# Neighbourhood attention: the last row group's bias tables from the host, the middle row groups head by head, scaling taken off GpSimd, and operand splits kept out of the steps that add tables

## The chip, the core and the metric

The kernel runs on one core of one Trainium2 chip. The metric is the device time of one execution in microseconds (us); lower is better. Engines are named as the profile names them: PE is TensorE (PEld its weight loads), DVE is VectorE, ACT is ScalarE, POOL is GpSimd, SP is SyncE, which here issues nearly all DMAs.

## What is computed

One layer of a bidirectional encoder: RMSNorm, one input projection to q, k, v and a gate, 2-D neighbourhood attention with a learned position bias, the SiLU gate, one output projection, the residual, and a final RMSNorm. Cut to what matters:

```python
S, D, H, hd, GRID_W = 2048, 1024, 16, 64, 64       # 32 rows of 64 tokens
h = rmsnorm(x, norm_0)
q, k, v, gate = split(h @ w_in_0, 4)                # 1024 -> 4096
for r in range(32):                                 # each grid row; keys of 8 rows, 16 columns
    s = einsum(q[r], k[rows(r)]) / sqrt(hd)
    s = where(col_valid, s + bias(rpb_0, r), -1e30)
    o[r] = einsum(softmax(s), v[rows(r)])
x = x + (o * silu(gate)) @ w_out_0                  # 1024 -> 1024
out = rmsnorm(x, norm_f)
```

All arrays are float32.

## The kernel before

**Products.** Matrix operands are split into a high and a low part in the fp32r type: ACT writes the high part (a copy), DVE writes the low part (the difference of the source and the high part, two inputs in SBUF). Each product is then three matmuls. In `use_item` the splits of projection weights are tiles `w` (L178, L179) and those of `w_out` are `woh`, `wol` (L183, L184). `split_og` splits the gated attention output, tile `ograw`, into `gh`, `gl` (L1107, L1108).

**Stages.** Two stages of seven-product projections come first (L419, L540); the change leaves them alone. From then on attention and the rest run together, in the loop `for i in range(N + 2)` at the end of `build`, of 66 steps. Queries are cut into four row groups T = 0 to 3 of 8 grid rows, heads into eight pairs p, so there are 32 (p, T), in the order of the list `order`; each takes two steps, a step being two of the four column blocks C. Row groups 1 and 2 have the same bias and mask; 0 and 3 have their own. So there are three row types, in `ROW_TYPE`.

A step i issues to PE, in this order:
- *fill*: matmuls of the last projections (L363 to L367), and after those, of the output projection (L1242 to L1246). `amount[i]` says how many matmuls, about 15 in the first 48 steps and 20 after.
- the transposes of pair i-2 (L1015), into PSUM banks `ph`. DVE and ACT copy them out as `pta` (L1019, L1018).
- the scores of pair i (L978), 12 matmuls into four banks `s`. Of the eight banks some were `ph` or output banks just before, so the second half of the scores starts only once the copies above, or the evictions `y` (L1140), have emptied them.
- the products with v of pair i-2 (L1033).

DVE adds the table `em` to the scores and takes the maximum (L985, with the L985 read of the accumulator); ACT takes the exponential (L988); DVE the reciprocal of the sum (L994); POOL multiplies by it (L996, `normalise`); the transposes of the next step wait for that.

**Tables.** `bias(p, ty, cty)` makes the six tables `em` of a head pair and a row type: POOL adds the laid-out bias `e` (one DMA of 240 KB per head, `load_e`) and the mask `mk` (L960). `begin(i)` calls it in the even steps in which the pair's tables aren't there. In `order` the first five pairs have T = 1 and 2 next to each other, the other three have all T = 1 before all T = 2, and so add their tables twice.

**The rest of the work.** `consume` splits weights some way ahead, twice in each group of 24 fill matmuls. `outputs` loads `ograw`, splits it ahead (`ahead`, with the distance `near`), and after 24 matmuls `add_rows` adds the residual (L1140) and squares on ACT (L1143). `finish` then takes the root of the row's mean square on DVE, eight small instructions L1156 to L1163, scales the left half on DVE (L1170) and the right half by ACT and POOL (L1171, L1172), and stores. `run_roots` issues those when `quiet` is set, that is, in odd steps.

Everything is issued in an order that the program writes out: `clock` counts fill matmuls, `store(key, lag, f)` puts f off by so many of them, `due` runs what has come due. DMAs of SP go in order.

Of the kernel before, what the change touches and what calls it, by code (L numbers as in the profile page):

```python
# [10 lines left out]
F32 = mybir.dt.float32  # L11
# [27 lines left out]
MASK_N = [[(u1 - u0) * (v1 - v0) for v0, v1 in TYPE_COLS] for u0, u1 in TYPE_ROWS]  # L39
MASK_ALL = sum(sum(n) for n in MASK_N)  # L40
KINDS = {"q": 0, "k": 4, "v": 8, "g": 12}
# [26 lines left out]
@with_exitstack  # L68
def build(ctx, tc, x, xr, xt, wg, rpb, w_out, n0, nf, masks, out):
    nc = tc.nc  # L70
# [199 lines left out]
    def load_ahead():  # L270
        while state["loaded"] < min(len(items), state["used"] + AHEAD):
            load_item(items[state["loaded"]])
            state["loaded"] += 1

    def consume(n, asked=False):
        for _ in range(n):
            load_ahead()
            if state["used"] == len(items) or not may_use(items[state["used"]]):
                return
            if items[state["used"]][0] == "o" and clock[0] - asked_at[items[state["used"]]] < 32 and not asked:  # L280
                return
            it = items[state["used"]]
            state["used"] += 1
            use_item(it)
# [69 lines left out]
    def group(w, a, c, n):  # L354
        p = bank(512, "pp")
        for k in range(NK):
            if k in (3, 6):
                consume(1)
# [533 lines left out]
    LAST, stored_at = {}, {}  # L892
    order = [(p, 0) for p in range(NP)] + [(p, T) for p in range(5) for T in (1, 2)]
    order += [(p, T) for T in (1, 2) for p in range(5, NP)] + [(p, 3) for p in range(NP)]
    pairs = [(p, T, (h, h + 1)) for p, T in order for h in (0, 2)]
# [56 lines left out]
    def bias(p, ty, cty):  # L952
# [4 lines left out]
        for s in range(2):  # L957
            t = mp([128, 512], F32, "em")[:, :n]
            EM[p, ty, cty, s] = t
            (nc.gpsimd if attending[0] or not s else nc.vector).tensor_tensor(  # L960
                sh(t), E[p, s][:, u0 + 4:u1 + 4, v0 + 8:v1 + 8].rearrange("p u (s v) -> p s u v", v=8), sh(MK[0][:, m0:m0 + n]), OP.add)

    X, PT, O, ST = {}, {}, {}, {}
# [150 lines left out]
    squared = [0]  # L1114
    quiet = [False]

# [31 lines left out]
    def finish(n):  # L1148
# [16 lines left out]
        def scale():  # L1165
# [3 lines left out]
            else:  # L1169
                nc.vector.scalar_tensor_tensor(y[0], y[0], r, late["nf"][0], op0=OP.mult, op1=OP.mult)  # L1170
                nc.scalar.activation(y[1], y[1], AF.Copy, scale=r)  # L1171
                nc.gpsimd.tensor_tensor(y[1], y[1], late["nf"][1], OP.mult)  # L1172

# [28 lines left out]
    def outputs():  # L1202
# [6 lines left out]
        def ahead(k, i=0):  # L1209
# [7 lines left out]
            n = ready["split"]  # L1217
            near = 2 if quiet[0] else 1 if i >= 4 else 0
            if n < ready["loaded"] and place[n] <= k + near and clock[0] - loaded_at[n] >= 28 and whole(n):
# [44 lines left out]
    first = 8  # L1264
    amount = [(early - 3 * first) / 48] * 48 + [(384 - 30) / 18] * 18
    calm_debt = amount[0] / 2
# [32 lines left out]
    def begin(i):  # L1299
        all_loads()  # L1300
        m = i // 2
        if i % 2 == 0 and i < N:
            load_v(*order[m])
        if i % 2 == 0 and i < N:
            p, T = order[m]
            ty = ROW_TYPE[T]
            for key in [key for key in EM if key[:2] != (p, ty)]:
                del EM[key]
            for cty in range(3):
                if (p, ty, cty, 0) not in EM:  # L1310
                    bias(p, ty, cty)
            if m + 1 < len(order):
                nx = order[m + 1]
                kh, kl = load_k(*nx)
                if nx[0] != p:
                    later_loads(load_e(nx[0]), 5, 3)
# [15 lines left out]
    for i in range(N + 2):  # L1332
        a = amount[i]
        begin(i)
        feed(a * 0.25)
        quiet[0] = i % 2 == 1 or i >= N
        if quiet[0]:
# [3 lines left out]
        feed(a * 0.55, 8)  # L1341
        quiet[0] = i >= N
        if 0 < i <= N:
# [53 lines left out]
```

## Time and profile before

| what | before |
|---|---|
| median of 3 runs (lowest to highest) | 1088.14 us (1086.99 to 1088.67) |
| the profiled execution | 1090.37 us |
| its span, first to last instruction | 1088.6 us |
| PE busy in the span | 1071.1 us (98%) |
| DVE, ACT, POOL busy | 724.2, 531.8, 355.7 us |
| attention loop, from its first fill matmul to the last instruction | 528 us to 1088.6 us |
| DMA | 205.39 MB, 189 GB/s over the span |

The profile's lines read: source line, engine, operation, written tile, arrow, read tiles, size, count; then busy time, mean of one in ns, and after the bar the idle time just before them with what ended most of it. In the list of waits a line reads "engine and line that waited, the one waited for: us in total, times, longest". In the timeline it is start, duration, engine, instruction, count, and in brackets the idle time of that engine just before. The windows give each engine's busy time in a stretch, with the count of instructions started there, then PE's granted clock, the DMA share and GB/s.

A matmul of 512 columns is shown with 389 ns, but the next one starts about 227 ns after it: the shown ends overlap. So a pause of PE shows in the starts, not in the busy share.

### The profile page before, as it was taken

Reading aid. Unit: us, or ns where it says so; the run is one execution under the profiler, and the core shown is the slowest. Engines: PE = TensorE matmul, PEld = TensorE weight load, DVE = VectorE, ACT = ScalarE, POOL = GpSimd, SP = SyncE. Lnnn points to the kernel's source line nnn. Section 1 sums busy time; section 2 is a strip of 40 time slices with the busy share of each in tenths; the row PEclk is TensorE's granted clock in tenths of the full one; section 3 lists DMA queues with packets and bytes.
Section 4 is the critical chain, followed back from the end, with each engine's and each line's share of the span. In section 5 each row is a group of like instructions: output and inputs, shape, how many; then the busy total and the mean of one; then the engine's idle time right before and its main releaser. Section 6 shows DMA issues by size and latency. Waiting matters only on the chain. (4 is left out here: it accounts for less than half of the span.)

```text
span 1088.6 us, 21531 instructions
## 1 busy us (share of the span) xinstructions
PE 1071.1 (98%) x7621; PEld 875.0 (80%) x7621; DVE 724.2 (67%) x1680; ACT 531.8 (49%) x1260; POOL 355.7 (33%) x474
## 2 busy tenths in 40 slices
PE   9999999999999999999999999999999999999997
PEld 6888888887888888888878888888878787888885
DVE  5376888769897536565675566657786757766553
ACT  7545344333343334332465565657666555655431
POOL 0000322212220000000175665544477656557210
PEclk9999999999999999999999999999999999999999
DMA  8633565444555234445997778858986777776352
GB/s 307 216 97 106 195 202 182 125 136 148 146 167 148 83 87 135 116 131 170 283 278 209 241 222 241 276 169 246 287 264 208 236 254 206 251 224 221 103 153 77
DMA packets 125299, 205.39 MB, mean 189 GB/s; under 512 B 11336, under 2 KB 51528, under 8 KB 125192
## 3 DMA queue, kind: packets, MB, share of 16 engines
q1 hardware_dynamic: 125048, 203.76, 60.7%
q8 instruction: 60, 0.98, 0.4%
q14 instruction: 47, 0.39, 0.1%
q10 hardware_dynamic: 144, 0.26, 0.1%
HBM read 145.26 MB, written 58.72 MB: 187 GB/s over the span
## 5 line engine op out<-in xcount | busy, mean ns | idle before, releaser
L960 POOL TENSOR_TENSOR em<-e,mk 128x480 f32<-128x480 f32 (+5 forms) x160 | 134.4, 878 | 192.6 <-DVE u L432 189.8
L996 POOL TENSOR_SCALAR x<-x,st 128x360 f32<-128x360 f32 (+5 forms) x256 | 142.5, 577 | 163.3 <-DVE st L994 110.4
L419 PE MATMUL pp<-h,f 128*128 128x512 f32 x576 | 186.5, 389 | 0.0
L988 ACT ACTIVATE x<-x,st 128x360 f32<-128x360 f32 (+5 forms) x256 | 151.7, 594 | 54.7 <-DVE st L985 54.7
L419 PE MATMUL pp<-t,f 128*128 128x512 f32 x648 | 156.0, 390 | 0.3 <-DVE u L432 0.2
L439 POOL TENSOR_TENSOR tmp<-tmp,rb 128x512 f32<-128x512 f32 x36 | 58.5, 1625 | 271.1 <-DVE tmp L437 220.3
L419 PEld LDWEIGHTS pp<-t,f 128*128 128x128 f32 x648 | 121.5, 188 | 26.4 <-DVE u L432 1.2
L419 PEld LDWEIGHTS pp<-h,f 128*128 128x128 f32 x576 | 108.1, 188 | 22.5
L985 DVE CUSTOM_DVE_ANT_0 x<-s,em 128x360 f32<-128x360 f32 (+5 forms) x256 | 123.7, 539 | 3.5 <-PE s L978 1.8
L419 PE MATMUL pp<-l,f 128*128 128x512 f32 x288 | 112.0, 389 | 0.0
L1019 DVE COPY pta<-ph 120x384 f32<-120x384 f32 (+5 forms) x128 | 62.9, 516 | 63.2 <-PE ph L1015 62.6
L1246 PE MATMUL po<-wol,gh 128*128 128x512 f32 x252 | 100.7, 399 | 0.0
L1033 PEld LDWEIGHTS o<-pta,vt 120*64 120x64 f32 (+2 forms) x1792 | 84.6, 138 | 19.8 <-issue 15.6
L1242 PE MATMUL po<-woh,gh 128*128 128x512 f32 x252 | 99.7, 396 | 0.0
L1244 PE MATMUL po<-woh,gl 128*128 128x512 f32 x252 | 99.5, 395 | 0.0
L1018 ACT ACTIVATE pta<-ph 120x384 f32<-120x384 f32 (+5 forms) x128 | 52.3, 459 | 88.5 <-PE ph L1015 88.4
L1033 PE MATMUL o<-pta,vt 120*64 120x128 f32 (+5 forms) x1792 | 93.5, 256 | 1.5 <-DVE pta L1019 1.2
L978 PE MATMUL s<-kt,qh 64*128 64x480 f32 (+5 forms) x512 | 86.8, 379 | 6.0 <-DVE pta L1019 2.3
L540 PE MATMUL pv<-wh,h 128*128 128x512 f32 x256 | 88.1, 390 | 0.0
L540 PE MATMUL pv<-wl,h 128*128 128x512 f32 x256 | 87.9, 389 | 0.0
L540 PE MATMUL pv<-wh,l 128*128 128x512 f32 x256 | 87.9, 389 | 0.0
L402 DVE TENSOR_TENSOR f<-raw,f 128x512 fp32r<-128x512 f32 x90 | 69.9, 776 | 22.4 <-ACT f L401 22.4
(149 smaller groups left out, 1910.3 us busy)
## 6 DMA issues: line engine op xcount, KB each, us to landing
raw<-in_wg_dram SPq DMA_DIRECT2D x126, 256.0 KB, 4.6
e<-in_rpb_dram SPq DMA_DIRECT2D x54, 240.0 KB, 4.2
row<-in_xr_dram SPq DMA_DIRECT2D x32, 256.0 KB, 4.2
vd<-v SPq DMA_DIRECT2D x32, 256.0 KB, 2.7
k_hi<-hi SPq DMA_DIRECT2D x32, 256.0 KB, 3.2
k_lo<-lo SPq DMA_DIRECT2D x32, 256.0 KB, 2.9
sgd<-sg SPq DMA_DIRECT2D x32, 256.0 KB, 3.2
qr<-qd SPq DMA_DIRECT2D x32, 256.0 KB, 3.6
```

The costliest lines, as they stand in the source:

```text
L402: nc.vector.tensor_tensor(t[:, 1], src, t[:, 0].bitcast(F32), OP.subtract)
L419: nc.tensor.matmul(B[n, P], t[:, int(m == 2), c], x[k][int(m == 1)], start=P in (1, 6, 5) and k == 0 and m == 0, stop=k == 3 and m == 2, s ...
L540: nc.tensor.matmul(ps[t], a[:, o], b, start=k == 0 and m == 0, stop=k == NK - 1 and m == 2)
L960: (nc.gpsimd if attending[0] or not s else nc.vector).tensor_tensor(sh(t), E[p, s][:, u0 + 4:u1 + 4, v0 + 8:v1 + 8].rearrange("p u (s v) - ...
L978: nc.tensor.matmul(pst[s], qq[a, qs], kk[a, :r1 - r0, c0:c1].rearrange("p r (s c) -> p s r c", c=8), start=(m == 0), stop=(m == 2))
L985: nc.vector.tensor_tensor_reduce(X[i, C][s], pst[s], EM[p, ROW_TYPE[T], COL_TYPE[C], s], -1.0, 1e38, OP.add, OP.min, st[:, s:s + 1])
L988: nc.scalar.activation(X[i, C][s], X[i, C][s], AF.Exp, bias=st[:, s:s + 1], scale=-1.0, accum_out=st[:, 2 + s:3 + s])
L996: nc.gpsimd.tensor_scalar(X[i, C][s], X[i, C][s], st[:, 4 + s:5 + s], 0.5, op0=OP.mult, op1=OP.mult)
L1033: nc.tensor.matmul(o[s * 64:s * 64 + 64, C * 128 + q0:C * 128 + q0 + nq], vt[:k, strip, s * 64:s * 64 + 64], t[:k, at:at + nq], start=firs ...
L1242: nc.tensor.matmul(p, gh, woh[q, j], start=(i == 0), stop=False)
L1244: nc.tensor.matmul(p, gl, woh[q, j], start=False, stop=False)
L1246: nc.tensor.matmul(p, gh, wol[q, j], start=False, stop=(i == NK - 1))
```

## The change

The host now adds bias and mask for row type 2 and passes them as `last`, 960 columns for each head; `load_last` reads the six tables of a head pair straight into the tiles `em`, 960 KB in six DMAs where `load_e` read 480 KB in two, and POOL adds nothing for T = 3. The order has T = 1 and T = 2 next to each other for all eight pairs. `finish` scales both halves on DVE, with neither ACT nor POOL. `quiet` is set in every step in which `begin` added no tables, not in odd steps, and `consume` and `ahead` split only then (unless the operand is needed at once); a group has three calls of `consume` instead of two. The first 48 steps have 60 fill matmuls less, the last 18 have 60 more.

```diff
-order = [(p, 0) for p in range(NP)] + [(p, T) for p in range(5) for T in (1, 2)]
-order += [(p, T) for T in (1, 2) for p in range(5, NP)] + [(p, 3) for p in range(NP)]
+order = [(p, 0) for p in range(NP)] + [(p, T) for p in range(NP) for T in (1, 2)] + [(p, 3) for p in range(NP)]
...
     def consume(n, asked=False):
         for _ in range(n):
             load_ahead()
+            if attending[0] and not quiet[0] and not asked:
+                return
...
-            if k in (3, 6):
+            if k in (1, 4, 7):
                 consume(1)
...
+    def load_last(p):
+        if p % 2:
+            ts = [mp([128, 512], F32, "em") for _ in range(6)]
+        else:
+            m = mkp([128, 3, 512], F32, "em")
+            ts = [ep([128, 512], F32, "em") for _ in range(4)] + [m[:, 0], m[:, 1]]
+        fs = []
+        at = 0
+        for cty, n in enumerate(MASK_N[2]):
+            for s in range(2):
+                EM[p, 2, cty, s] = t = ts.pop(0)[:, :n]
+                fs.append(lambda t=t, a=at, n=n, s=s: nc.sync.dma_start(t, last[2 * p + s, :, a:a + n]))
+            at += n
+        return fs
...
-                nc.vector.scalar_tensor_tensor(y[0], y[0], r, late["nf"][0], op0=OP.mult, op1=OP.mult)
-                nc.scalar.activation(y[1], y[1], AF.Copy, scale=r)
-                nc.gpsimd.tensor_tensor(y[1], y[1], late["nf"][1], OP.mult)
+                for j in range(2):
+                    nc.vector.scalar_tensor_tensor(y[j], y[j], r, late["nf"][j], op0=OP.mult, op1=OP.mult)
...
-            near = 2 if quiet[0] else 1 if i >= 4 else 0
+            near = 2 if quiet[0] else -1
...
-    amount = [(early - 3 * first) / 48] * 48 + [(384 - 30) / 18] * 18
+    kept = 60
+    amount = [(early - kept - 3 * first) / 48] * 48 + [(384 + kept - 30) / 18] * 18
...
     def begin(i):
         all_loads()
         m = i // 2
+        quiet[0] = True
         if i % 2 == 0 and i < N:
             p, T = order[m]
+            load_v(p, T)
             ty = ROW_TYPE[T]
             for cty in range(3):
                 if (p, ty, cty, 0) not in EM:
                     bias(p, ty, cty)
+                    quiet[0] = i == 0
             if m + 1 < len(order):
                 nx = order[m + 1]
                 kh, kl = load_k(*nx)
-                if nx[0] != p:
+                if nx[1] == 3:
+                    later_loads(load_last(nx[0]), 1, 1.5)
+                elif nx[0] != p:
                     later_loads(load_e(nx[0]), 5, 3)
```

How the order of instructions moves, at three places. First DVE in step 36, where before the tables of a pair are added by POOL; `x` and `st` are scores and their maxima, `og` the gated output, `y` an evicted output row:

```order
L985 ISA x_8908,st<-s_8892,em 128x360
L985 ISA st 128x1
L1049 TENSOR_TENSOR og<-o,sgt 128x512
L184 TENSOR_TENSOR wol<-raw,woh 128x512
L1140 TENSOR_TENSOR y<-po,xr 128x512
L184 TENSOR_TENSOR wol<-raw,woh 128x512
L994 RECIPROCAL st<-st 128x2 x2
L1019 COPY pta<-ph_8992 120x4x64
L1019 COPY pta<-ph_9007 120x6x64
```

After, a step of the middle row groups with tables, step 40, has the same instructions of attention:

```order
L1004 ISA x_9296,st<-s_9280,em 128x360
L1004 ISA st 128x1
L1068 TENSOR_TENSOR og<-o,sgt 128x512
L1158 TENSOR_TENSOR y<-po,xr 128x512
L1013 RECIPROCAL st<-st 128x2 x2
L1038 COPY pta<-ph_9363 120x4x64
L1038 COPY pta<-ph_9378 120x6x64
```

The two splits `wol` ahead of the copies `pta` are gone from such a step; they stand in steps without tables, among others 37, 38, 41 and 42.

Second, DVE in a step with roots ahead of the copies. Before, step 45 has two roots (the second ends here), the split of the queries, and two scalings:

```order
L1162 SCALAR_TENSOR_TENSOR st_9442<-st_9442 128x1
L1163 SCALAR_TENSOR_TENSOR st_9442<-st_9442 128x1
L505 SCALAR_TENSOR_TENSOR ql<-qr,qh 128x512
L1170 SCALAR_TENSOR_TENSOR y<-y,st_9205,acc_162 128x512
L1170 SCALAR_TENSOR_TENSOR y<-y,st_9442,acc_162 128x512
L994 RECIPROCAL st<-st 128x2 x2
L1019 COPY pta<-ph_10103 120x6x64
L1019 COPY pta<-ph_10120 120x6x64
```

After, the first root comes in step 46, alone (its last three instructions are shown; `og` and the other five stand ahead), with both halves of its row:

```order
L1179 SCALAR_TENSOR_TENSOR st_9336<-st_9336 128x1
L1180 SCALAR_TENSOR_TENSOR st_9336<-st_9336 128x1
L1181 SCALAR_TENSOR_TENSOR st_9336<-st_9336 128x1
L1189 SCALAR_TENSOR_TENSOR y<-y,st_9336,acc_162 128x512
L1189 SCALAR_TENSOR_TENSOR y<-y,st_9336,acc_163 128x512
L1013 RECIPROCAL st<-st 128x2 x2
L1038 COPY pta<-ph_10083 120x4x64
L1038 COPY pta<-ph_10098 120x6x64
```

One root and two scalings stand ahead of the copies now, where two roots, a split and two scalings stood.

Third, POOL in the last row group, before:

```order
L996 TENSOR_SCALAR x_10542<-x_10542,st 128x384
L960 TENSOR_TENSOR em<-e,mk 128x288 x2
L960 TENSOR_TENSOR em<-e,mk 128x384 x2
L960 TENSOR_TENSOR em<-e,mk 128x288 x2
L996 TENSOR_SCALAR x_10667<-x_10667,st 128x384
L996 TENSOR_SCALAR x_10668<-x_10668,st 128x384
L996 TENSOR_SCALAR x_10674<-x_10674,st 128x288
L996 TENSOR_SCALAR x_10675<-x_10675,st 128x288
L1172 TENSOR_TENSOR y<-y,acc_163 128x512
```

and after:

```order
L1015 TENSOR_SCALAR x_10525<-x_10525,st 128x384
L1015 TENSOR_SCALAR x_10526<-x_10526,st 128x384
L1015 TENSOR_SCALAR x_10532<-x_10532,st 128x288
L1015 TENSOR_SCALAR x_10533<-x_10533,st 128x288
L1015 TENSOR_SCALAR x_10676<-x_10676,st 128x288
```

POOL has only the normalising left there.

More of the change, by code (lines that the diff above doesn't have):

```diff
@@ L39 @@
 MASK_N = [[(u1 - u0) * (v1 - v0) for v0, v1 in TYPE_COLS] for u0, u1 in TYPE_ROWS]
-MASK_ALL = sum(sum(n) for n in MASK_N)
+MASK_ALL = sum(sum(n) for n in MASK_N[:2])
+LAST_ALL = sum(MASK_N[2])
 KINDS = {"q": 0, "k": 4, "v": 8, "g": 12}
@@ L68, in build @@
 @with_exitstack
-def build(ctx, tc, x, xr, xt, wg, rpb, w_out, n0, nf, masks, out):
+def build(ctx, tc, x, xr, xt, wg, rpb, last, w_out, n0, nf, masks, out):
     nc = tc.nc
@@ L273, in load_ahead @@
             state["loaded"] += 1
+    quiet = [False]
     def consume(n, asked=False):
@@ L1114, in build @@
     squared = [0]
-    quiet = [False]
     def add_rows(n, j, ps):
@@ L1301, in begin @@
         m = i // 2
-        if i % 2 == 0 and i < N:
-            load_v(*order[m])
+        quiet[0] = True
         if i % 2 == 0 and i < N:
             p, T = order[m]
+            load_v(p, T)
             ty = ROW_TYPE[T]
-            for key in [key for key in EM if key[:2] != (p, ty)]:
-                del EM[key]
             for cty in range(3):
@@ L1335, in build @@
         feed(a * 0.25)
-        quiet[0] = i % 2 == 1 or i >= N
         if quiet[0]:
@@ L1341, in build @@
         feed(a * 0.55, 8)
-        quiet[0] = i >= N
         if 0 < i <= N:
@@ L1373 @@
                       axis=1)
+    masks = mask_table()
+    u0, u1 = TYPE_ROWS[2]
+    last, at = [], MASK_ALL
+    for (v0, v1), n in zip(TYPE_COLS, MASK_N[2]):
+        t = spread.reshape(H, 128, 15, 32)[:, :, u0 + 4:u1 + 4, v0 + 8:v1 + 8]
+        t = t.reshape(H, 128, u1 - u0, (v1 - v0) // 8, 8).transpose(0, 1, 3, 2, 4).reshape(H, 128, n)
+        last.append(np.where(masks[:, at:at + n] == 0, t, np.float32(NEG)))
+        at += n
     w = np.asarray(inputs["w_in_0"]).reshape(NK, 128, NU, 256).transpose(2, 1, 0, 3)
@@ L1382 @@
         "rpb": np.ascontiguousarray(spread),
+        "last": np.ascontiguousarray(np.concatenate(last, axis=2)),
         "w_out": np.ascontiguousarray(np.asarray(inputs["w_out_0"])),
@@ L1385 @@
         "nf": np.ascontiguousarray(np.asarray(inputs["norm_f"])),
-        "masks": mask_table().astype(ml_dtypes.bfloat16),
+        "masks": masks[:, :MASK_ALL].astype(ml_dtypes.bfloat16),
     }
```

## The prediction

> **What bounds the kernel now.** I read the page first.
>
> ```profile
> PE 1071.1 (98%) x7621; PEld 875.0 (80%) x7621; DVE 724.2 (67%) x1680; ACT 531.8 (49%) x1260; POOL 355.7 (33%) x474
> L960 POOL TENSOR_TENSOR em<-e,mk 128x480 f32<-128x480 f32 (+5 forms) x160 | 134.4, 878 | 192.6 <-DVE u L432 189.8
> L1172 POOL TENSOR_TENSOR y<-y,acc 128x512 f32<-128x512 f32 x15 | 20.6, 1371 | 92.2 <-ACT y L1171 82.9 <-DVE st L994 9.4
> ```
>
> PE works almost without a pause, and the change leaves the count of its matmuls as it is. So only PE's pauses can be won or lost. Removing 66 of the 160 table sums (18 in the middle groups, 48 in the last), some 58 us of POOL, is worth nothing as busy time. The question is who waits for what.
>
> So next the waits of PE's weight loads, by stretch of the attention loop (528 to 562, 780 to 830, 830 to 890, 890 to 1000 us).
>
> ```profile
> PEld s L978 <- DVE lo L350: 0.6, 1, 0.6
> PEld o L1033 <- DVE pta L1019: 0.6, 1, 0.6
> ...
> PEld s L978 <- DVE y L1140: 1.9, 1, 1.9
> PEld s L978 <- DVE pta L1019: 1.3, 2, 0.9
> ...
> PEld s L978 <- ACT pta L1018: 2.0, 1, 2.0
> PEld o L1033 <- DVE pta L1019: 1.3, 1, 1.3
> ...
> PEld s L978 <- DVE pta L1019: 2.3, 2, 1.5
> ```
>
> These are 1.2 + 3.2 + 3.3 + 2.3 = 10.0 us, in nine places, and all are of one kind: the scores or the products with v wait until DVE or ACT has emptied a bank.
>
> Then the timeline at the three largest. Around 793 us (step 36):
>
> ```profile
> 790.95 5.52 POOL L960 TENSOR_TENSOR em<-e,mk 128x360 f32<-128x360 f32 x6
> 793.18 3.84 DVE L184 TENSOR_TENSOR wol<-raw,woh 128x512 fp32r<-128x512 f32 x1 [1.13 <-ACT woh L183]
> 796.94 0.68 DVE L1140 TENSOR_TENSOR y<-po,xr 128x512 f32<-128x512 f32 x1
> 797.54 0.68 DVE L184 TENSOR_TENSOR wol<-raw,woh 128x512 fp32r<-128x512 f32 x1
> 797.67 0.50 PE L978 MATMUL s<-kt,qh 64*128 64x480 f32 x1 [1.60 <-DVE y L1140]
> ```
>
> The split `wol` takes 0.68 us alone, but 3.84 us while POOL adds tables: it ends a little after POOL's last sum (790.95 + 5.52 = 796.47). Behind it DVE's eviction `y` and the copies wait, and PE with them.
>
> At 862 us (step 45) and 898 us (step 49) POOL scales `y`:
>
> ```profile
> 864.56 2.42 DVE L1170 SCALAR_TENSOR_TENSOR y<-y,st,acc 128x512 f32<-128x512 f32 x2
> 864.92 1.51 POOL L1172 TENSOR_TENSOR y<-y,acc 128x512 f32<-128x512 f32 x1 [1.30 <-ACT y L1171]
> 865.27 1.17 PE L978 MATMUL s<-kt,qh 64*128 64x360 f32 x4 [1.51 <-ACT pta L1018]
> ...
> 898.37 1.46 POOL L1172 TENSOR_TENSOR y<-y,acc 128x512 f32<-128x512 f32 x1 [6.53 <-ACT y L1171]
> 898.60 1.77 DVE L505 SCALAR_TENSOR_TENSOR ql<-qr,qh 128x512 fp32r<-128x512 f32 x1
> 901.68 0.41 PE L978 MATMUL s<-kt,qh 64*128 64x288 f32 x2 [1.29 <-DVE pta L1019]
> ```
>
> Every DVE instruction that is long here reads two tiles in SBUF while POOL works on two; evictions from PSUM beside the same sums keep their 0.7 us. So these pauses come from POOL stretching DVE just ahead of the copies.
>
> At step 45 something more follows:
>
> ```profile
> 858.41 1.44 PE L1033 MATMUL o<-pta,vt 120*64 120x128 f32 x28
> 867.63 2.62 PE L1033 MATMUL o<-pta,vt 120*64 120x128 f32 x28 [0.88 <-DVE pta L1019]
> 865.65:872.48 6.83, 5.95 (x40) 4.88 (x40) 5.14 (x14) 2.62 (x8) 6.00 (x9) 0.50 0.27 85
> ```
>
> From 865.65 us the granted clock is 0.50 for 6.83 us. The 28 products with v take 2.62 us instead of 1.44. PE is busy 5.95 us of it, so the half clock cost between 1.2 us (those products alone) and 3.0 (half of 5.95). I take 2.6, near the upper end, since scores and fill lie in it too.
>
> **The change part by part, against the profiled execution's 1090.37 us.**
>
> *Sums and splits apart (middle groups).* No split is issued in a step with sums, so the 3.84 us split at step 36 is 0.68, and the small pauses after it go too: -3.2 us. Next late would be the copies behind the splits' own DVE work. In the changed order steps 37 and 38 hold seven and six DVE instructions besides the attention's, at some 0.6 us each, beside 20 and 15 fill matmuls. The nearest row is step 35 before, with the same mixture:
>
> ```profile
> 786.52 0.39 PE L1242 MATMUL po<-woh,gh 128*128 128x512 f32 x1
> 786.75 0.39 PE L1244 MATMUL po<-woh,gl 128*128 128x512 f32 x1
> 787.07 0.80 PE L1015 MATMUL ph<-ident,x 64*120 64x64 f32 x20
> 788.58 0.64 PE L978 MATMUL s<-kt,qh 64*128 64x360 f32 x4
> 790.71 0.50 PE L1246 MATMUL po<-wol,gh 128*128 128x512 f32 x1
> ...
> 785.84 1.29 DVE L1108 TENSOR_TENSOR gl<-ograw,gh 128x512 fp32r<-128x512 f32 x2
> 787.04 1.29 DVE L184 TENSOR_TENSOR wol<-raw,woh 128x512 fp32r<-128x512 f32 x2
> 788.25 0.22 DVE L994 RECIPROCAL st<-st 128x2 f32<-128x2 f32 x2
> 788.38 1.00 DVE L1019 COPY pta<-ph 120x384 f32<-120x384 f32 x2
> ...
> L985 DVE CUSTOM_DVE_ANT_0 x<-s,em 128x360 f32<-128x360 f32 (+5 forms) x256 | 123.7, 539 | 3.5 <-PE s L978 1.8 <-POOL x L996 0.2
> ```
>
> There PE goes through with no bracket, that is, with no wait: fill matmuls start 0.23 us apart, and attention's part lasts 790.71 - 787.07 = 3.6 us, its second half of scores starting 1.5 us in. Step 38 is tighter: its DVE work is six times 0.6 and about 3.4 for attention (four maxima of 0.54, two copies 1.0, reciprocals 0.2), 7.0 us, beside 15 x 0.23 + 3.6 = 7.1 of PE. I take +0.7 us for steps 37 to 42, between 0 and 3.2 (the whole pause moved there).
>
> *No scaling on POOL.* The rows of the scaling (shortest, median, longest in ns) and of a root's first and last instruction, of eight:
>
> ```profile
> L1170 DVE SCALAR_TENSOR_TENSOR y<-y,st,acc x15: 740/750/1815, 846.6 to 1073.3; 128x512 f32<-128x512 f32 x15
> 928.55 0.21 DVE L1156 TENSOR_SCALAR st<-st 128x1 f32<-128x1 f32 x1
> 930.06 0.16 DVE L1163 SCALAR_TENSOR_TENSOR st<-st 128x1 f32<-128x1 f32 x1
> ```
>
> POOL loses 15 instructions (20.6 us) and ACT 15, none on the path. DVE gains 15 scalings of 0.75 us, 11.3 us. The pauses at steps 45, 49 and 53 go: -3.3 and -2.3. What is next late: in step 46 DVE now has `og` (0.7), one root (928.55 to 930.22, 1.7), two scalings (1.5) and the reciprocals (0.2) ahead of the first copy (0.5), beside only 11 fill matmuls. That is 4.6 us, and some 0.2 for the last maximum. PE reaches the second half of the scores after 11 x 0.23 + 0.2 + 1.5 = 4.2. So +0.6 us there, 0 to 2. In the last 18 steps DVE has 0.75 us more for an output row, which two steps of 8 us or more make, with no stretching: +0.6 for all, 0 to 3.
>
> *Clock.* I hold the slow stretch to be a consequence of the pause, since PE was idle for 1.5 us of the window just before it. It goes with it: -2.6 us.
>
> *Last group's tables by DMA.* Two steps move 960 KB of tables instead of two `e` of 240 KB.
>
> ```profile
> e<-in_rpb_dram SPq DMA_DIRECT2D x54, 240.0 KB, 4.2
> 880.00:992.00 112.00, 110.26 (x1133) 90.02 (x1132) 76.96 (x249) 64.23 (x183) 69.18 (x103) 1.00 0.72 226
> 688.00:704.00 16.00, 16.00 (x163) 13.01 (x161) 9.70 (x31) 10.63 (x29) 8.26 (x12) 1.00 0.97 306
> ```
>
> The 112 us from 880 us hold seven pairs of steps: 16.0 us and 16.0 x 226 = 3.6 MB each. Now 0.5 MB more of tables, and an estimated 0.2 for 6 more fill matmuls beside 40 (their share of the loads and stores, held to be under half of the 3.6): 4.3 MB in 16.0 + 6 x 0.23 = 17.4 us, 247 GB/s. 306 GB/s ran for 16 us with no wait of PE, and tables are loaded two steps ahead. So 0; if that cover fails, see the rivals. SP gets four issues more per pair; behind them are keys needed two steps later: 0.
>
> *Middle groups side by side; 60 matmuls later.* PE's work is only moved. Row group 1 ends four steps later than before, so its first outputs are loaded and split close to use, in steps 48 to 50: +0.4 us, 0 to 2. Steps of the first 48 shrink by 1.25 matmuls (0.28 us), and POOL's six sums (5.5 us at 790.95) stay well inside two steps.
>
> *Start (528 to 562 us).* Step 2 loses its weight splits, but the key evictions behind one of its pauses stay: I take half of 1.2, -0.6 us; 0 to 1.2.
>
> Sum: -3.2 - 3.3 - 2.3 - 2.6 - 0.6 = -12.0; +0.7 + 0.6 + 0.6 + 0.4 = +2.3; together -9.7, from 1090.37 to 1080.7 us. The profiled execution stands 2.2 us above the median of 1088.14. That is near the slow clock's 2.6 us: if the other runs didn't have it, the gain from the median is 7.1 (1081.0); if they had, 9.7 (1078.4). I forecast 1080.0 us, about halfway.
>
> **The rivals.**
>
> *A: the pauses move (0.15).* DVE gets 11 us more work and the splits are pressed into fewer steps; steps 37 to 42, 46 and 48 to 57 pause by the upper bounds, +3.2 + 2 + 3 + 2 = 10.2 instead of 2.3. For it: DVE is 99% filled in step 38 by my count. Against it: step 35. Time: 1080.0 + 7.9 = 1087.9; halfway is 1084.
>
> *B: the slow clock stays (0.08).* Only one pause of its kind was followed by it; those at 797.67 and 901.68 us were not. So it may belong to where a window of the clock's control falls, and hit a step with few fill matmuls (7 in two steps after the change) without a pause. Then 2.6 us remain: 1080.0 + 2.6 = 1082.6. The Trainium skill, TensorE: Matmul & The Clock Gate, section "HAM oscillation — how this bites in real kernels", puts the danger at idle gaps of PE of more than about 3.4 us; by that rule 1.5 us of idling would not have lowered the clock, the stretch would have another cause, and it would stay. The trace speaks against the limit, not for it: no gap of that length stands ahead of 865.65 us.
>
> *C: the tables' DMA becomes the bound, slower (0.07).* If the last group's mixture, with rows of 1152 to 1536 bytes, gets no more than the 226 GB/s that the trace shows on average from 880 to 992 us, two steps take 4.3 / 0.226 = 19.0 us instead of 17.4, 1.6 us for each of eight pairs, 13 us: 1080 + 13 = 1093. It decides from under 247 GB/s on. Against it: that average was demand, not a limit, and 306 stands above it.
>
> **How the numbers follow.** Forecast 0.70, A 0.15, B 0.08, C 0.07. 0.2% of the time, 2.2 us, is about what a measurement of this kernel can tell from no change; so faster means under 1086.0, slower over 1090.3. The forecast's own unknowns run from -2.9 (no new pause, 2.3, and the start's other 0.6) to some +4, which is 1077 to 1084; 1078.4, if every run had the slow clock, lies in it. The range takes in B and most of A: 1075.5 to 1087.5; C and the tails are left out. Faster: 0.70 + 0.08 + half of A and a little = 0.85; same 0.08; slower 0.07.
>
> **What would show it.** Right: no wait of PE on `y` or `pta` over 1 us from 780 to 1000 us; `wol` and `ql` all near 0.7 us; the clock 1.00 throughout; at most 1 us of pause at step 46. Wrong: scores waiting on DVE in steps 37 to 42 by several us (A), a stretch at 0.50 (B), DVE's maxima waiting on a DMA of `em` (C), or PE waiting on `gh` or `gl` in fill, which nothing before shows.

## The result and the profile after

The changed kernel takes 1081.09 us (median of 6 runs, 1080.29 to 1081.56), the kernel before 1088.26 us beside it (1085.94 to 1088.67): a ratio of 0.9938, 95% interval 0.9925 to 0.9951, 7.2 us less. The profiled executions stand 9.0 us apart, 1081.33 us against 1090.37. The forecast was 1080.0 us, with a range of 1075.5 to 1087.5.

First the page of the changed kernel: the engines, and the group of the table sums.

```profile
PE 1068.0 (99%) x7621; PEld 872.9 (81%) x7621; DVE 721.4 (67%) x1695; ACT 520.1 (48%) x1245; POOL 278.4 (26%) x393
...
L964 POOL TENSOR_TENSOR em<-e,mk 128x264 f32<-128x264 f32 (+3 forms) x94 | 77.1, 853 | 191.6 <-DVE u L437 189.8
```

POOL has lost 77 us, 66 table sums and 15 products, and PE's count is what it was. Then the waits of PE's weight loads on DVE and ACT, from 520 to 562 us (first fence) and from 780 to 1000 us (second), where before there were waits of up to 2.0 us on `y` and `pta`.

```profile
PEld s L997 <- DVE st L1004: 1.3, 1, 1.3
...
PEld s L997 <- ACT pta L1037: 0.4, 1, 0.4
```

```profile
PEld o L1052 <- DVE st L1004: 1.5, 5, 0.3
PEld s L997 <- ACT pta L1037: 0.7, 2, 0.4
PEld o L1052 <- DVE pta L1038: 0.7, 2, 0.4
PEld o L1052 <- ACT pta L1037: 0.4, 1, 0.4
PEld s L997 <- DVE pta L1038: 0.4, 1, 0.4
```

From 780 to 1000 us no single wait is longer than 0.4 us (the third number). The long one is at the start: the scores of step 1 wait 1.3 us for DVE's maxima.

The splits of `w_out` and the scalings have their short durations everywhere (groups of DVE from 780 to 1000 us), and the windows show the clock at 1.00 and DMA at 263 GB/s in the last group, against 226 before.

```profile
L1189 DVE SCALAR_TENSOR_TENSOR y<-y,st,acc 128x512 f32<-128x512 f32 x18 | 12.7, 746 | 0.1
...
L185 DVE TENSOR_TENSOR wol<-raw,woh 128x512 fp32r<-128x512 f32 x11 | 7.4, 685 | 1.1 <-ACT woh L184 1.1
```

```profile
880.00:992.00 112.00, 111.99 (x1088) 91.88 (x1085) 78.28 (x253) 60.03 (x174) 26.93 (x52) 1.00 0.83 263
...
562.00:1020.00 458.00, 457.69 (x4825) 373.42 (x4824) 307.36 (x972) 269.87 (x754) 202.50 (x325) 1.00 0.78 243
```

PE is busy 457.69 of 458.00 us. So every sign that the prediction named as "right" is there. That shows that the pauses are gone; it doesn't show why. The experiments had to tell.

**Theories.** *Stretch* is the prediction's: POOL's work on two SBUF tiles makes DVE's work on two SBUF tiles longer, just ahead of the copies PE waits for; the change pulls them apart. Its rival, *queue*: POOL hardly matters; PE pauses in a step in which DVE has more to do ahead of the copies than PE has fill. A third, *clock*: the stretch at half clock belongs to its place and not to a pause.

A step's pause below is worked out from the timeline: the time from the step's first score matmul behind the last transposes to its first product with v, and from there to the next fill, less the same times in neighbouring steps (1.49 and 1.37 us in the middle groups, 1.23 and 1.37 in the last).

### The profile page after: what moved, and what is told of

It is laid out like the page before. It is cut to its first block, busy times and chain, and to the rows that moved or that the text cites. A ratio compares the mean times of both kernels' runs of the same rounds, so it can differ in the third digit from the quotient of the medians.

```text
span 1079.5 us, 21403 instructions
## 1 busy us (share of the span) xinstructions
PE 1068.0 (99%) x7621; PEld 872.9 (81%) x7621; DVE 721.4 (67%) x1695; ACT 520.1 (48%) x1245; POOL 278.4 (26%) x393
## 4 chain that ended last, share of the span: by engine, by line
PE 95%; DVE 3%; ACT 1%; issue 1%; POOL 0%; DVEq 0%; POOLq 0%; ACTq 0%
PE pp L424 29%; PE pv L545 16%; PE o L1052 8%; PE s L997 8%; PE po L1263 6%; PE po L1259 6%; PE po L1261 5%; PE ph L1034 4%; PE pp L372 4%; PE pp L368 4%; PE pp L370 4%; DVE f L407 1%; PE zp L1278 1%; ACT x L1007 0%; DVE raw L413 0%
## 5 line engine op out<-in xcount | busy, mean ns | idle before, releaser
L964 POOL TENSOR_TENSOR em<-e,mk 128x264 f32<-128x264 f32 (+3 forms) x94 | 77.1, 853 | 191.6 <-DVE u L437 189.8
```

## Experiments: one part of the change put into the kernel before

All ratios are to the kernel before on the same chip.

**Scaling on DVE only.**

```diff
-                nc.vector.scalar_tensor_tensor(y[0], y[0], r, late["nf"][0], op0=OP.mult, op1=OP.mult)
-                nc.scalar.activation(y[1], y[1], AF.Copy, scale=r)
-                nc.gpsimd.tensor_tensor(y[1], y[1], late["nf"][1], OP.mult)
+                for j in range(2):
+                    nc.vector.scalar_tensor_tensor(y[j], y[j], r, late["nf"][j], op0=OP.mult, op1=OP.mult)
```

> The kernel before with one part of the change: both halves of a finished output row are scaled on DVE, nothing of it on ACT and POOL; order, tables and splits are those of before. Theory (POOL's work on two SBUF tiles stretches DVE's work on two SBUF tiles just ahead of the copies): the pauses of steps 45, 49 and 53 go (3.3 + 2.3 us) and with the first of them the half clock (2.6 us); DVE has 11 us more work, some 1 us of it seen. So 5 to 7 us less than before, a wol of 3.8 us stays in step 36 and PE pauses there as before (2.9 us). Rival queue (PE waits because too much stands in DVE's and ACT's queues ahead of the copies, POOL has no part in it): DVE's queue gets longer by 0.75 us a row, so no gain or up to 2 us slower. Rival clock (the half clock belongs to a place in the kernel, not to the pause): it stays, and the gain is 3 us or less.

Measured: 1084.68 us, ratio 0.9962 (0.9949 to 0.9976), 4.0 us less. But the large pause is still there. Step 45 in the timeline (PE, DVE and POOL; the roots are L1156 to L1163, scaling L1171 here):

```profile
857.37 0.21 DVE L1156 TENSOR_SCALAR st<-st 128x1 f32<-128x1 f32 x1
...
858.97 0.20 DVE L1156 TENSOR_SCALAR st<-st 128x1 f32<-128x1 f32 x1
...
860.56 0.69 DVE L505 SCALAR_TENSOR_TENSOR ql<-qr,qh 128x512 fp32r<-128x512 f32 x1
...
861.17 2.73 DVE L1171 SCALAR_TENSOR_TENSOR y<-y,st,acc 128x512 f32<-128x512 f32 x4
...
863.82 0.22 DVE L994 RECIPROCAL st<-st 128x2 f32<-128x2 f32 x2
863.96 1.00 DVE L1019 COPY pta<-ph 120x384 f32<-120x384 f32 x2
864.17 2.38 POOL L996 TENSOR_SCALAR x<-x,st 128x360 f32<-128x360 f32 x4 [8.12 <-DVE st L994]
...
864.55 1.52 PE L1033 MATMUL o<-pta,vt 120*64 120x128 f32 x28 [2.58 <-DVE pta L1019]
```

POOL stood idle for 8.12 us, and all of DVE's instructions have their short durations. Still PE waits 2.58 us: DVE has two roots, `ql` and four scalings, 6.6 us from 857.37 to 863.96, ahead of the copies, and the step has 9 fill matmuls, 2.0 us. So at step 45 the pause needs no stretch, and queue stands. The half clock follows again, for 3.41 us.

For the kernel before this doesn't clear POOL. There DVE took 7.2 us from the first root to the copies (859.83 to 867.04 us), and 1.9 of them are two stretched places: one instruction of the second root, 1.15 us for 0.22, and the two scalings, 2.42 for 1.40. Here the two scalings more, 1.3 us, stand in their place. ACT carried a part of it too, in before:

```profile
862.35 1.28 POOL L1172 TENSOR_TENSOR y<-y,acc 128x512 f32<-128x512 f32 x1 [3.35 <-ACT y L1171]
862.50 1.15 DVE L1161 SCALAR_TENSOR_TENSOR st<-st 128x1 f32<-128x1 f32 x1
...
864.12 0.72 ACT L1171 ACTIVATE y<-y,st 128x512 f32<-128x512 f32 x1 [1.86 <-DVE st L1163]
...
864.75 0.74 ACT L1018 ACTIVATE pta<-ph 120x384 f32<-120x384 f32 x2
```

ACT's scaling waits 1.86 us for the second root, and ACT's copies, for which PE first waits (1.51 us), stand behind it. With the scaling on DVE alone ACT copies at 860.29 us and that wait is gone; the one for DVE's copies remains.

Step 36, whose instructions are the same as before, shows the other surprise: POOL's sums, DVE's split and the eviction.

```profile
790.92 6.40 POOL L960 TENSOR_TENSOR em<-e,mk 128x360 f32<-128x360 f32 x6
...
793.15 1.10 DVE L184 TENSOR_TENSOR wol<-raw,woh 128x512 fp32r<-128x512 f32 x1 [1.13 <-ACT woh L183]
...
794.17 0.68 DVE L1140 TENSOR_TENSOR y<-po,xr 128x512 f32<-128x512 f32 x1
```

Before, the sums took 5.52 us and the split 3.84. Here the sums take 6.40 and the split 1.10, and PE loses 0.5 us instead of 2.9. The same two instructions meet, but the other one gives way; the eviction `y`, which reads PSUM, keeps its 0.68 us beside the sums. Three more profiled kernels with these instructions in step 36 came out in the mild way; they are named below.

**Splits only in steps without sums.**

```diff
+            if attending[0] and not quiet[0] and not asked:
+                return
...
-            if k in (3, 6):
+            if k in (1, 4, 7):
...
-            near = 2 if quiet[0] else 1 if i >= 4 else 0
+            near = 2 if quiet[0] else -1
```

`quiet` is set as in the changed kernel.

> The kernel before with one part: operands are split only in steps that add no tables (three chances in a group in place of two); scaling, order and tables are those of before. Theory: step 36 has no wol beside POOL's sums, so its pause of 2.9 us goes, some 0.5 us may come in steps 37 and 39, which get the splits; steps 45, 49 and 53 stay as they were, since those pauses come from the scaling, and so does the half clock. About 2.5 us less than before (1 to 3.5). The start may lose up to 1 us, as in the changed kernel, since step 1 has four splits beside 15 fill matmuls. Rival queue: the splits only move from step to step, the sum of pauses stays: 0 plus or minus 1 us.

Measured: 1089.69 us, ratio 1.0007 (0.9991 to 1.0022). Step 36 has no pause, but step 51 has one of 1.8 us where there was none, step 61 one of 0.9, and step 1 one of 1.0. The pauses moved, as queue says: in the order of before every even step from 36 to 62 adds tables, so roots and splits still meet in the odd ones. In step 51 a product of POOL has a part in it: DVE's scaling beside it takes 1.59 us instead of 0.75.

**Order only.**

```diff
-    order = [(p, 0) for p in range(NP)] + [(p, T) for p in range(5) for T in (1, 2)]
-    order += [(p, T) for T in (1, 2) for p in range(5, NP)] + [(p, 3) for p in range(NP)]
+    order = [(p, 0) for p in range(NP)] + [(p, T) for p in range(NP) for T in (1, 2)] + [(p, 3) for p in range(NP)]
```

> The kernel before with one part: row groups 1 and 2 of all eight head pairs side by side, so 18 table sums fewer on POOL; splits, scaling and last group's tables as before. Theory: what counts is not how many sums there are but whether one meets a split or a scaling ahead of the copies. In this order step 36 has no sums any more while it still has a wol, so its pause (2.9 us) goes; sums stand in steps 40 and 44, without splits. Steps 45, 49, 53 keep the scaling on POOL, so their pauses stay. About 2 to 3 us less than before; up to 1 us may come back at steps 47 and 48, where the first outputs of row group 1 are loaded late. Rival queue: the same number of splits and copies stands in DVE's queue, 0 plus or minus 1 us.

Measured: 1100.24 us, ratio 1.0099 (1.0077 to 1.0122), 11 us slower: a miss of every theory. The waits from 870 to 905 us tell why.

```profile
PE po L1241 <- ACT gh L1106: 9.8, 1, 9.8
...
ACT gh L1106 <- DMA ograw<-ogd: 8.1, 1, 8.1
```

Row group 1 ends four steps later, its gated output is written at 884.2 us, read back from 888.2 us on and landed at 896.5, and until then no fill is left. PE stands still for 9.8 us in step 47, waiting for data that earlier were there long ago. The expectation was also wrong that step 36 has no sums in this order: the same head pair begins there, and POOL adds its six tables (6.39 us). The step shows the mild outcome again (0.5 us).

**Last group's tables from the host only.** The diff is `load_last` and what calls it, as shown above.

> The kernel before with one part: the last row group's tables come laid out from the host by DMA, so 48 table sums fewer on POOL from step 47 on, and 0.5 MB more of DMA for each head pair; order, splits and scaling as before. Theory: in the last group the pauses were 2.3 us, at steps 49 and 53, from POOL's scaling with sums queued about it; steps 36 and 45 are untouched, so 6.2 us of pause and the half clock stay. The scaling remains, so at most 1 us is won: 0 to 1 us less than before. Rival sums (every one of POOL's sums costs something beside DVE's work, wherever it stands): 48 of the 66 sums removed would bring some 70 percent of the whole gain, 5 us. Rival C of the prediction (the tables' DMA is the bound): slower by up to 13 us.

Measured: 1088.23 us, ratio 0.9995 (0.9976 to 1.0014): no change, as stretch said and against the rival of the sums. The 0.5 MB more of DMA for each head pair cost nothing either. Step 36: 0.5 us. Step 49 pauses 1.7 us as in before, and here a half clock of 3.41 us follows it, which before doesn't have (last section).

**60 fill matmuls put off, nothing else.**

```diff
-    amount = [(early - 3 * first) / 48] * 48 + [(384 - 30) / 18] * 18
+    kept = 60
+    amount = [(early - kept - 3 * first) / 48] * 48 + [(384 + kept - 30) / 18] * 18
```

> The kernel before with nothing but 60 fill matmuls put off: 1.25 fewer in each of the first 48 steps, 3.3 more in each of the last 18. Order, tables, splits, scaling and roots are those of before, so POOL does all its sums and its 15 products. The roots and scalings of the first output rows then fall into steps 47 to 49 with 14 to 23 fill matmuls, where before they fell into step 45 with 9. Theory fill (PE pauses where DVE's roots, scalings and copies of a step exceed PE's fill): the pauses of steps 45, 49 and 53 shrink to 1 to 2 us in all and the half clock of 6.8 us goes: 5 to 7 us less than before, about 1082.5. Theory stretch (the prediction's: POOL's work beside DVE's makes the pauses): POOL still adds tables in each of these steps and scales, so at least half of the pauses stay and the gain is 3 us or less.

Measured: 1089.98 us, ratio 1.0004 (0.9989 to 1.0019). Step 45's pause and its half clock are gone as the theory of fill said, yet nothing is won: step 2, into which four weight splits now fall, pauses 2.2 us, with a half clock of 6.83 us behind it; and step 49 pauses 2.9. Its rows:

```profile
880.95 2.39 DVE L1108 TENSOR_TENSOR gl<-ograw,gh 128x512 fp32r<-128x512 f32 x2
...
881.15 3.32 POOL L1172 TENSOR_TENSOR y<-y,acc 128x512 f32<-128x512 f32 x2 [4.35 <-ACT y L1171]
...
883.26 1.76 DVE L505 SCALAR_TENSOR_TENSOR ql<-qr,qh 128x512 fp32r<-128x512 f32 x1
...
884.95 0.68 DVE L1140 TENSOR_TENSOR y<-po,xr 128x512 f32<-128x512 f32 x1
...
885.68 0.64 PE L978 MATMUL s<-kt,qh 64*128 64x384 f32 x3 [1.16 <-DVE y L1140]
```

Here stretch is real: beside POOL's two products the two `gl` take 2.39 us and `ql` 1.76, where 1.29 and 0.69 are their own durations, 2.2 us more in a step that pauses 2.9. PE waits for the `y` and the copies behind them.

**Scaling on DVE, and roots in any step.** As the first kernel, and:

```diff
-        if quiet[0]:
-            run_roots()
+        run_roots()
```

> The kernel before with both halves scaled on DVE, and with the roots taken in any step once they are due, where before they wait for the next odd step. With the scaling on DVE alone (1084.7 us) PE still waited 2.6 us in step 45 on the copies, and the clock was 0.50 for 3.4 us after it: DVE had two roots of 1.6 us and four scalings of 0.7 us ahead of the copies there, beside only 9 fill matmuls. Theory now (a queue too long at one place): with one of the roots in step 44, which has 22 fill matmuls, step 45 has one root and two scalings, the pause and the half clock go, and 3 to 4 us are won on top: about 1081. Theory of the prediction (POOL's work beside DVE's makes the pause): nothing of POOL's is changed, so the time stays at 1084.7, within 0.7.

Measured: 1083.76 us, ratio 0.9953 (0.9941 to 0.9966), some 0.9 us less than with the scaling alone where 3 to 4 were expected. Step 45 has no pause, as expected; step 42 has one instead, of 1.7 us, and the half clock behind it costs 1.6. It now has the first root, beside 8 fill matmuls and six sums (rows of POOL and DVE):

```profile
834.54 5.50 POOL L960 TENSOR_TENSOR em<-e,mk 128x360 f32<-128x360 f32 x6
...
837.35 0.15 DVE L1158 TENSOR_SCALAR st<-st 128x1 int32<-128x1 int32 x1
837.54 0.86 DVE L1159 SCALAR_TENSOR_TENSOR st<-st 128x1 f32<-128x1 f32 x1
838.44 0.80 DVE L1160 SCALAR_TENSOR_TENSOR st<-st 128x1 f32<-128x1 f32 x1
839.28 0.79 DVE L1161 SCALAR_TENSOR_TENSOR st<-st 128x1 f32<-128x1 f32 x1
840.10 0.16 DVE L1162 SCALAR_TENSOR_TENSOR st<-st 128x1 f32<-128x1 f32 x1
```

Instructions on a single column take 0.8 us each while the sums run, and 0.16 from the end of the sums on (834.54 + 5.50 = 840.04); L1158, with one tensor operand, keeps its 0.15. Each two-input instruction waits out about one of POOL's (0.92 us each), however small it is itself. The Trainium skill, GPSIMD Engine Reference, section "Key points", says that POOL contends with DVE's instructions that have two SBUF inputs; the trace agrees, and in these rows the price goes by POOL's instruction, not by DVE's.

So neither theory stands alone: DVE's queue of a step, its own work and what POOL adds to it, against that step's fill. The next kernels ask which part of the change settled it.

## Experiments: one part taken out of the changed kernel

**Old scaling back** (the first diff, reversed).

> The changed kernel with the old scaling: left half on DVE, right half by ACT and POOL. No table sums stand near the scaling any more, roots are spread over the steps, and the fill is thicker (21 to 27 matmuls). Theory stretch: each of POOL's 15 products still meets DVE's work on two SBUF tiles and holds it up by about 0.7 us; where the copies stand right behind, PE pauses: slower by 1 to 3 us (1082 to 1084). Theory queue: DVE has 11 us less to do, no pause comes: the same or up to 0.7 us faster (1080.4 to 1081.4).

Measured: 1080.28 us, ratio 0.9922 (0.9909 to 0.9934): not slower than the changed kernel (0.9925 to 0.9951). POOL's line of products (shortest, median, longest in ns) and who waited for it:

```profile
L1190 POOL TENSOR_TENSOR y<-y,acc x15: 1290/1295/1617, 854.3 to 1063.4; 128x512 f32<-128x512 f32 x15
...
who waited for it (us, times):
  PEld ph L1034: 0.4, 1
```

They are there, all 15, and PE waits 0.4 us for them in all. The change's largest term by the prediction brings nothing once the rest is in.

**Splits in every step.**

```diff
-            if attending[0] and not quiet[0] and not asked:
-                return
...
-            near = 2 if quiet[0] else -1
+            near = 2
```

> The changed kernel with splits allowed in every step, those with table sums too; all else, the fill, the order and the roots, as in the changed kernel. Theory stretch: a split that meets POOL's sums takes either some 1.1 us or, if POOL keeps going first, up to 3.8 us, and where copies stand behind it PE pauses; splits meet sums in the steps of 36, 40 and 44 at most, so 0 to 4 us slower, with more spread from execution to execution (1081 to 1085). Theory queue: it lengthens no queue by more than a split of 0.7 us, so within 0.7 us of the changed kernel's 1081.1; the steps 37 and 41, which held seven and six splits beside 20 fill matmuls, lose a little of their pauses.

Measured: 1081.54 us, ratio 0.9933 (0.9919 to 0.9946). The same time as the changed kernel; step 36 pauses 0.9 us and step 39 0.5, step 37 no longer.

**Tables of the last group added on POOL again** (48 sums more; splits and roots still allowed in those steps).

```diff
-                if nx[1] == 3:
-                    later_loads(load_last(nx[0]), 1, 1.5)
-                elif nx[0] != p:
+                if nx[0] != p:
...
-                    quiet[0] = i == 0
+                    quiet[0] = i == 0 or T == 3
```

> The changed kernel with the last row group's tables added on POOL again (48 sums more, no tables by DMA); splits, roots and scaling stay allowed in those steps, so all of DVE's work in the last 18 steps is as in the changed kernel and meets the sums. Theory stretch (the prediction's): gl, ql and the scalings of each pair of steps take 1.5 to 3 us longer beside six sums, and where a root or a copy stands behind them PE pauses, as it did for 2.9 us in step 49 with the fill alone put off: 3 to 8 us slower than the changed kernel's 1081.1. Theory fill (with 21 to 27 fill matmuls and one root a step DVE's queue is short enough): the stretched work is covered, 0 to 1 us slower.

Measured: 1080.91 us, ratio 0.9931 (0.9918 to 0.9945), no difference. `gl` there takes 721 ns in the mean against 685: the sums seldom meet it. So this kernel says that the sums cost nothing where they stand, not that they would cost nothing under a split.

**Roots only in odd steps.**

```diff
-        if quiet[0]:
+        if i % 2 or i >= N:
             run_roots()
```

> The changed kernel with the roots of output rows only in odd steps, as before the change. Step 49 then has two roots and five instructions on y on DVE, beside 23 fill matmuls and without table sums or work of POOL on y. Theory fill: 2 x 1.6 + 5 x 0.7 + ql 0.7 + reciprocals 0.2 and the first copy 0.5 make some 8 us in front of PE's second half of scores, which it reaches after 23 x 0.23 + 1.7 = 6.9 us and what was left over from step 48: a pause of 0.5 to 2 us in step 49, perhaps 0.5 in step 47, so 0.5 to 2.5 us slower than 1081.1; if the pause passes 2.5 us the clock falls to 0.50 behind it, 1.5 to 3 us more. Theory stretch: without POOL's work no pause, within 0.5 of 1081.1.

Measured: 1080.42 us, ratio 0.9927 (0.9915 to 0.9939). No difference, though step 49 has two roots and four scalings again (and the expectation's 2.5 us for the half clock is no limit that a run shows: in step 42 above it followed a wait of 1.3 us):

```profile
872.84 0.21 DVE L1174 TENSOR_SCALAR st<-st 128x1 f32<-128x1 f32 x1
...
876.03 0.69 DVE L510 SCALAR_TENSOR_TENSOR ql<-qr,qh 128x512 fp32r<-128x512 f32 x1
876.64 0.69 DVE L1158 TENSOR_TENSOR y<-po,xr 128x512 f32<-128x512 f32 x1
877.24 2.73 DVE L1189 SCALAR_TENSOR_TENSOR y<-y,st,acc 128x512 f32<-128x512 f32 x4
...
880.02 1.00 DVE L1038 COPY pta<-ph 120x384 f32<-120x384 f32 x2
```

This is the pair that tells most, though the two steps lie in different row groups. DVE works 7.2 us here from the first root to the copies (872.84 to 880.02), with 23 fill matmuls in the step, and PE pauses 0.25 us. In step 45 of the kernel with the scaling alone it was 6.6 us, with 9 fill matmuls, and 2.6 to 2.8 us of pause. The 14 matmuls between them are 14 x 0.23 = 3.2 us.

**No fill held back.**

```diff
-    kept = 60
+    kept = 0
```

> The changed kernel with no fill matmuls held back (60 in the changed kernel). Side by side the middle row groups end row group 1 four steps later; when the order alone was changed, PE stood still for 9.8 us in step 47, waiting for the output rows of row group 1 to be written, read back (8.1 us) and split. Theory: the 60 matmuls are what covers this; without them the fill runs out as there, two roots fall into step 45 with its 9 matmuls as before, and the time is some 10 to 14 us longer than the changed kernel's: 1091 to 1095. Rival (the 9.8 us came from the queues of the old splits and scaling, not from missing fill): it stays within 2 us of the changed kernel.

Measured: 1097.47 us, ratio 1.0079 (1.0065 to 1.0093), 16 us slower than the changed kernel. PE waits 11.4 us in step 47 for the outputs of row group 1, as with the order alone:

```profile
PE po L1259 <- ACT gh L1126: 11.4, 1, 11.4
PE o L1052 <- DVE pta L1038: 2.6, 1, 2.6
```

The second line is step 45: with its 9 fill matmuls back and two roots in it, the 2.6 us pause is back too, without any of POOL's scaling and with the split rule in force. POOL is idle for 8.8 us there, and DVE takes 6.6 us from the first root to the copies, as with the scaling alone. With the half clock behind it this step costs some 5.5 us. The greater part of the 16 us is the wait in step 47 and the half clock that goes with it, a cost that the new order brings and that the 60 matmuls cover.

**Two chances for a split, with the old scaling.**

```diff
-            if k in (1, 4, 7):
+            if k in (3, 6):
```

> The changed kernel with the old scaling on ACT and POOL (which gave 1080.28 us), and with two chances for a split in a group of fill, in the places of before, in place of three. In the changed kernel step 1 has four weight splits beside 15 fill matmuls, and steps 1 to 3 pause 2.5 us in all; here step 1 has two beside 22, and two more come in step 2. If the pauses of the start come from those four splits, step 1's 1.4 us go and step 2's stay at 0.8 to 1.1: 0.5 to 1.5 us less than with the old scaling alone, 1079 to 1080. If they come from the key evictions and the first maxima alone, the time stays at 1080.3.

Measured: 1080.93 us, ratio 0.9918 (0.9898 to 0.9939), against 0.9922 without this edit. Step 1's pause of 1.4 us is gone, as expected, but splits come later in the middle, step 35 pauses 0.6 us, and the time is not lower. None of these kernels is separable from the changed one; the one with the old scaling is as fast with less changed.

## Why the prediction was right, and where it wasn't

The time, the sign and the list of new pauses held. The reasons held in part. Between the two profiled executions the sum said 9.7 us and 9.0 came, each term within some 0.6 us but for the start. That the medians, 7.2 us apart, fit as well is partly luck: the forecast halved a doubt about which runs had the half clock, and the doubt lay elsewhere (next paragraph).

*Sums and splits apart (-3.2).* Between the two profiled executions it is what happened: all `wol` take 0.68 to 0.69 us, step 36 has no pause. But the 2.9 us were one outcome of an unsettled meeting: the kernels with the scaling, the order, the tables, and the scaling and roots alone each show 0.5 us at that step. So the term was mis-sized for the median, and the split rule brought nothing, alone or last. This is also where the profiled execution's 2.2 us above the median most likely came from. The prediction gave them to the half clock; but that was in every one of the six profiled kernels that had step 45's pause, so it can hardly have been missing in the other runs. That the outcome changes from run to run of one kernel was not shown.

*No scaling on POOL (-3.3 and -2.3).* The pauses of steps 45, 49 and 53 went, as the sum had it. The step that failed is the sentence "So these pauses come from POOL stretching DVE just ahead of the copies". At step 45 DVE's own queue of 6.6 us makes a pause of 2.6 us with POOL idle, and in the changed kernel POOL's scaling costs nothing. The stretch was real, 1.9 of DVE's 7.2 us there in the profile of before, but taking it away put two more scalings in its place; at step 49 with the fill alone put off it was 2.2 us of a pause of 2.9. So it is one part of DVE's queue, and what it costs goes by the step's fill. The first 1.51 us of PE's wait at step 45 in before, put down to ACT in the prediction's row, came from ACT's scaling, which waited for the second root ahead of ACT's copies; the prediction left that out. Alone, this part is worth 4.0 us; by the profiles 1.3 of it lies at steps 45 and 46, 1.4 at 49 and 53, and the rest isn't placed.

*Middle groups side by side; 60 matmuls later (+0.4).* Here stood "PE's work is only moved". This term was needed for the gain, though it doesn't bring it alone: with the 60 matmuls the first output rows, with their roots and scalings, fall into steps of 11 to 27 fill matmuls, where before two rows met in step 45 with its 9. Taken out, step 45's 5.5 us of pause and half clock come back; put alone into the kernel before, it won nothing, since the pauses at steps 2 and 49 grew. And it is a cover that I did not name: without it, the new order costs 9.8 to 11.4 us of waiting for `ograw`. The 0.4 us itself was too high: steps 48 to 50 pause 0.1 us.

*Clock (-2.6).* Right in cause, and near in size: by the starts of steps 45 and 46 it cost 2.2 us. The half clock came and went with the pauses: with step 45's in six kernels, at step 42 and at step 2 where the pause was there, behind the standstill of step 47 in two, and nowhere from 530 to 1020 us in the changed kernel and the five without a large pause. Rival B falls. But not every pause has it: step 49's 1.7 us is followed by it with the last group's tables alone, and not in before. So for pauses of that length it is in part luck. The rule quoted from the Trainium skill, TensorE: Matmul & The Clock Gate, section "HAM oscillation — how this bites in real kernels", that the danger lies in gaps of more than about 3.4 us, doesn't hold here (last section).

*Start (-0.6).* Wrong in sign. Step 2 lost 0.3 us, step 3 0.2, but step 1 got 1.4: three chances a group press four weight splits beside 15 fill matmuls, ahead of the maxima. I had counted step 2 alone.

*New costs.* Steps 37 to 42: 0.7 foreseen, 0.8 found (0.41 of it in step 37, 0.22 in 41). Step 46: 0.6 foreseen, none found. The last 18 steps: 0.6 foreseen, about 0.8 found, 0.35 of it at step 58. Tables by DMA: 0 foreseen; 263 GB/s ran with PE at 111.99 of 112.00 us, above the 247 from which rival C would have decided, and taking the tables away again changed nothing.

*Rival A* came true in the parts alone (the splits moved their pauses to steps 51 and 61, the 60 matmuls theirs to 2 and 49), and not in the whole.

What stays open: whether the order and the 60 matmuls alone, put into the kernel before, give the whole gain. The changed kernel can spare each of the other four parts one at a time; that it can spare them together was not tried, and neither was the changed kernel with the old order.

## What to carry to other kernels

Where one engine must never wait, count for each step what the other engines have queued ahead of the instruction it waits for, and set that against the work it has in that step: here 2.6 us of pause stood beside 9 matmuls of independent work, and 0.25 us beside 23, with a queue of 6.6 and 7.2 us. Moving that work is no cure by itself, since the 60 matmuls alone won nothing. Take a change apart from both ends: put alone, five of its parts gave between -4 and +11 us; of the five taken out alone, four made no difference and one was needed. And a long instruction in one profile that meets another engine's may be one of two outcomes: look at the same place in a second kernel before putting its price into a sum.

## What the runs showed of the hardware

*The clock.* The windows of 3.41 us ahead of and in some half-clock stretches; the first number after the length is PE's busy time, 1.00 or 0.50 the granted clock. In before (the first two rows were followed by full clock, the third by half):

```profile
793.97:797.38 3.41, 2.10 (x31) 1.38 (x30) 3.41 (x2) 0.00 (x0) 2.50 (x3) 1.00 1.07 304
899.78:903.19 3.41, 2.12 (x31) 1.62 (x30) 3.41 (x11) 0.98 (x4) 1.93 (x5) 1.00 0.36 100
862.24:865.65 3.41, 1.90 (x31) 1.34 (x29) 3.27 (x8) 1.40 (x4) 2.00 (x2) 1.00 0.89 353
```

With the scaling on DVE alone, and with the roots in any step:

```profile
862.36:865.77 3.41, 1.22 (x28) 1.22 (x28) 3.41 (x10) 0.21 (x1) 1.60 (x3) 1.00 0.43 149
865.77:869.18 3.41, 3.41 (x14) 2.62 (x11) 1.85 (x7) 2.42 (x8) 3.41 (x5) 0.50 0.58 144
```

```profile
838.81:842.23 3.42, 2.11 (x22) 1.26 (x19) 3.31 (x13) 1.13 (x3) 2.77 (x5) 1.00 1.00 269
842.23:845.64 3.41, 3.41 (x31) 3.02 (x26) 2.52 (x8) 2.77 (x9) 0.87 (x2) 0.50 0.85 328
```

With the last group's tables alone, followed by half clock:

```profile
895.51:898.92 3.41, 2.15 (x34) 1.62 (x30) 3.41 (x9) 0.77 (x2) 1.92 (x4) 1.00 0.30 58
```

The transitions lie on a grid of 3.41 us (the stretches at 0.50 last 3.41, 6.83, 10.24 or 13.65 us). In the 14 profiles, from 530 to 1020 us, each window at full clock in which PE was idle for 1.5 us or more was followed by half clock in the next one or more (nine of nine); with 1.26 to 1.31 us idle two of four were; with less, none. So here PE idle for some 40% of one window was enough, in one piece or two; just below it, idle time alone doesn't settle it, as the 1.29 us of before's second row and the 1.26 us of the last row show. By the starts of the matmuls, a stretch of 3.41 us behind a pause cost some 1.6 us and one of 6.83 us 2.2 to 2.9. At step 36 a gap of 1.60 us was cut by a boundary into 1.31 and 0.29, and cost nothing more.

*Which engine gives way.* When DVE's split and POOL's sums met at step 36, the split took 3.84 us and the sums 5.52 in one execution; 1.10 and 6.40 in another. I had taken the first for the rule.
